# A two-layer hybrid backbone on one core: two tiles of tokens instead of one gather their experts in the second layer

## The chip, the core and the metric

The kernel runs on one core of a Trainium2 chip. The metric is the device time of one execution in microseconds (us); each time shown is the median of three timed runs. A separate execution is recorded by the hardware profiler, and all rows below come from that one.

## What is computed

Two layers over 512 latent tokens of width 1024, with 256 context tokens in front. Each layer has four mixers side by side (RG-LRU, RWKV-7, mLSTM, Hyena), then the expert part, PEER. The first layer computes context and latents (768 tokens), the second the latents alone (512 tokens). The change lies in the expert part of the second layer, which computes, cut to what matters:

```
def token_block(xb):                                   # h: the normed, modulated tokens
    q = (xb @ wq).reshape(T, 8, 2, 128)
    s = einsum('thcq,hckq->thck', q, keys)             # 8 heads, 2 halves, 128 keys each
    sv, si = top_k(s, 16)
    cand = sv[:, :, 0, :, None] + sv[:, :, 1, None, :] # 16 x 16 pairs of every head
    top_s, top_j = top_k(cand.reshape(T, 8, 256), 16)
    eidx = ...                                         # 8 x 16 = 128 experts of 16384 per token
    gate = softmax(top_s)
    act = gelu(einsum('td,thkd->thk', xb, U[eidx]))
    return einsum('thk,thkd->td', gate * act, V[eidx])
```

## The kernel before

Engines in short: PE is TensorE, DVE VectorE, ACT ScalarE, POOL GpSimd, SP the engine that only issues transfers. The second layer is `l = 1` in the code; every table of numbers has an entry for each layer, `X[l]`. A tile is 128 tokens; the second layer has four.

The expert part treats tokens in two ways.

- **Dense tiles.** All 16384 rows of U are multiplied with the tile's tokens on PE, in 128 products of 128 rows each (`s_part`), the gelu of the result goes to DRAM (`Ad`). A U product is: load 128 rows (`ur`), split them on ACT and DVE into a high and a low part (`uh`, `ul`), 24 matmuls (8 blocks of 128 features, 3 each for the parts), as many columns wide as there are dense tokens (`Wd`). The gates that routing chose are spread over all experts by `build` (comparisons and products on DVE, small matmuls on PE) and go to DRAM (`Gd`). Later come 128 V products: load `Ad`, `Gd` and 128 rows of V, multiply the first two (`gm`), split V and the result into high and low parts (`pv`), 24 matmuls into eight PSUM banks that gather over all 128 products.
- **Gathered tiles.** For each of the 128 experts of a token, a gather (an indirect DMA that POOL issues, line 1527) fetches row e of U for all 128 tokens into a buffer `grow` of 512 KB; DVE multiplies it with the tokens and sums (a U use, line 1500). Then 128 gathers fetch rows of V, and DVE adds each, times its weight, to a sum (a V use, line 244). A tile costs 256 gathers and 256 uses.

`choose(n, after)` paces the gathers. At each call it puts the uses of the rows whose call lies `LAG[l] = 2` calls back, then copies n columns of indices (`at`, on DVE), then issues n gathers, each into one of `GBUF[l]` buffers `grow`. The calls are laid in by hand: in `s_ahead` after each U product (`CHS`), in `build` (`CHN`), in `trailing` (`CHT`), and in the loop over V products, where n is what is left over the products that are left, until `CHE = 128`:

```
choose(min(8, (NS - done[0]) // max(1, CHE - j)), ins)
```

Before the change the second layer has `NG = 1` gathered tile, so three dense ones (384 columns), and `CUT = 0`: all 512 tokens are scored together (16 half heads, `scores`), then the gathered tile is routed first, then each dense tile is routed and built. `s_ahead(NSP[1][1] = 3)` puts three U products ahead of each quarter of a build; what is left of the 128 U products then runs in `trailing`, one gather beside each. The first layer has `NG = 2`, `CUT = 1` and 512 dense columns already: there the tokens are normed and scored in two pieces, the gathered tiles are scored and routed first, and the dense ones follow with gathers beside them.

The program's order on each engine comes from a scheduler at build time. Engines run their instructions in that order; a DVE instruction that waits holds up all behind it.

I call the stretch from the first routing matmul to the end of the U products the U stage, and what follows up to the end of the V products and uses the V stage.

Of the kernel before, what the change touches and what calls it, by code (L numbers as in the profile page):

```python
# [13 lines left out]
A = mybir.AluOpType  # L14
AF = mybir.ActivationFunctionType
X = mybir.AxisListType.X
PSUM, DRAM = bass.MemoryType.PSUM, bass.MemoryType.DRAM
# [3 lines left out]
EPS = 1e-6  # L21
# [5 lines left out]
# ---------------------------------------------------------------- layout on the host  # L27
# [90 lines left out]
def consts():  # L118
    o = {}
    for n, L in (("l", SEQ), ("c", CTX)):  # L120
        # Half of the times and of the frequencies: e and o below are the sums and differences of the tokens t and
        # their mirror images, of which the even and the odd frequencies need one each for cosine and sine.
        # 0: the filters, t against L - t; 1, 2: tokens, t + 1/2 against L - t - 1/2, and back.
# [73 lines left out]
NSP = ((5, 5, 6), (6, 3, 6))  # L197
# [8 lines left out]
GBUF = (4, 6)  # L206
CHN = (1, 6)
NG = (2, 1)
TOK = (2, 1)
CHS = ((1, 2), (200, 0))  # L210
CUT = (1, 0)
# [3 lines left out]
# ---------------------------------------------------------------- the program  # L215

def body(tc, I, out, dbg=None, stop=None):
# [56 lines left out]
    def segs(n):  # L274
        """columns in PSUM banks: the latents' 512, then the context's 256 before them"""
        return [(max(0, n - 512), n)] + ([(0, n - 512)] if n > 512 else [])

    with pool("keep") as kp, pool("scr", space=DRAM) as dp:
        # ---------------------------------------------------------- persistent
# [13 lines left out]
        def inv_sqrt(o, i, scale, eps_ap_or_val):  # L293
            """(i * scale + eps) ** -0.5"""
            act(o, i, AF.Ln, scale, eps_ap_or_val)
            act(o, o, AF.Exp, -0.5)
# [10 lines left out]
        # ---------------------------------------------------------- modulation vectors  # L307
        def ada(l, rounds, wp, pp, cs, dma, bufs):
            """columns 2048 * r on; the two vectors' products lie on partitions 32 * q and 32 * q + 1"""
# [23 lines left out]
        # ---------------------------------------------------------- Hyena's filters  # L333
        def dft_part(p, n, L, kind, f):
            """two parts each of the cosines and sines of 128 frequencies"""
# [6 lines left out]
        def sin_(p, t, ps, frq, bias, L):  # L342
            """sin(frq * (ps + bias)) with the argument brought to [-pi, pi]"""
# [13 lines left out]
        def spectrum(l, n, L, p, pp, dst_):  # L357
# [12 lines left out]
            # the first half of the times on the upper partitions; the second, mirrored and with the middle in the  # L370
            # place of time L, on the lower ones
# [10 lines left out]
            # forward plus and minus backward, each the sum (0) and difference (1) of a time and its mirror image  # L382
# [34 lines left out]
            # 1 / (L * (sum of the absolute values + EPS)); 1/L = 2/N is the weight of a frequency in the inverse  # L417
# [5 lines left out]
            for f in range(NC):  # L423
# [15 lines left out]
                if f == 0:  # L439
                    # the highest frequency, in the place of the sine of frequency 0  # L440
# [16 lines left out]
        # ---------------------------------------------------------- prologue  # L457
# [18 lines left out]
        # ---------------------------------------------------------- shared pieces  # L476
        def rms_scale(p, pp, srcs, n, tag, tags=(("sq", 2), ("rstd", 1))):
            """1 / sqrt(mean of squares over all rows + EPS), on every partition"""
# [14 lines left out]
        def norm_mod(hps, p, pp, x, l, which, t0, tag, cut=None):  # L493
            """what the products read, in two parts; for the tokens before and from cut on in a pool each"""
# [16 lines left out]
        def projector(wp, pp, src, tag, off=0, ks=range(8), eng=None):  # L511
            """rows of a product with h for the tokens from t0 on, by segments; early(c) fetches a row's weights"""
# [26 lines left out]
        def padded(p, zd, c, tag, bufs, t0):  # L539
            """a row block of z with two zeros before and one behind each stream, in three stretches of 256 tokens"""  # L540
# [12 lines left out]
        def conv(o, xp, taps, bias, t0):  # L553
            """o = sum of w * (token + shift) + bias; the first tap carries the bias"""
# [26 lines left out]
        # ---------------------------------------------------------- RG-LRU  # L581
# [1263 lines left out]
```

## Time and profile before

| | |
|---|---|
| median of three runs | 4984.07 us (4979.75 to 5007.8) |
| profiled execution, its span | 5021.4 us |
| expert part of the second layer in it | 3545 to 5005 us: U stage to 4437, V stage after it |
| busy over the span | PE 91%, DVE 72%, ACT 35%, POOL 27% |

The span runs from the first to the last instruction of the profiled execution; of that execution no other time is given. PE's busy time counts matmuls that overlap in the array, so it says that PE was rarely without one, not that it was at its peak. The share over the whole span mixes stages with different limits, so the stages of the expert part are read apart.

### The profile page before, as it was taken

How to read it: one execution, taken by the hardware profiler on the slowest of the kernel's cores; microseconds unless marked ns; L12 is line 12 of the kernel's file. 1: busy time of each engine (PE TensorE's matmuls, PEld its weight loads, DVE VectorE, ACT ScalarE, POOL GpSimd, SP SyncE). 2: the span in 40 equal slices, each digit the busy share in tenths (PEclk: the TensorE clock that was granted, in tenths of full speed). 3: DMA queues.
4: the chain of work that ended last, by engine and by line, in shares of the span. 5: the costliest groups of instructions: out<-in, count | busy, mean ns of one | idle time of the engine just before them, and what ended most of it. 6: DMA issues, size and time to landing. Idle time of an engine off the chain costs nothing. (4 is left out here: it accounts for less than half of the span.)

```text
span 5021.4 us, 66832 instructions
## 1 busy us (share of the span) xinstructions
PE 4590.8 (91%) x24203; PEld 3842.1 (77%) x24203; DVE 3624.9 (72%) x7303; ACT 1777.9 (35%) x2546; POOL 1375.8 (27%) x1117
## 2 busy tenths in 40 slices
PE   7879898799899999799999887898899998999998
PEld 3658567688777888687788665787688898999997
DVE  5772647399788897688889677556589875567777
ACT  4352222353233444322222335212534443333333
POOL 1211111002344454234455222000002332323332
PEclk9889999899999999899999898968999999999999
DMA  4442545346688999899999544203426889888896
GB/s 177 160 137 77 189 161 158 143 130 236 225 298 307 322 329 332 311 352 353 362 379 381 178 152 134 68 19 110 140 80 231 269 284 345 286 283 325 321 328 248
DMA packets 521083, 1170.01 MB, mean 233 GB/s; under 512 B 68192, under 2 KB 250272, under 8 KB 516272
## 3 DMA queue, kind: packets, MB, share of 16 engines
q1 hardware_dynamic: 227440, 563.42, 32.5%
q0 software_dynamic: 134912, 484.06, 27.2%
q10 hardware_dynamic: 158400, 118.25, 7.3%
q8 instruction: 191, 3.13, 0.3%
q14 instruction: 140, 1.15, 0.1%
HBM read 992.95 MB, written 173.02 MB: 232 GB/s over the span
## 5 line engine op out<-in xcount | busy, mean ns | idle before, releaser
L254 PE MATMUL d.S<-mrg.hhi,d.ul 128*128 128x512 f32 (+1 forms) x2048 | 772.6, 377 | 85.4 <-DVE d.ul L251 76.2
L1527 POOL DMA_INDIRECT d.grow<-in_V_dram,d.at x369 | 578.7, 1568 | 712.2 <-DVE d.at L1522 562.4
L254 PE MATMUL d.S<-mrg.hlo,d.uh 128*128 128x512 f32 (+1 forms) x2048 | 760.2, 371 | 0.1
L254 PE MATMUL d.S<-mrg.hhi,d.uh 128*128 128x512 f32 (+1 forms) x2048 | 757.6, 370 | 0.0
L254 PE MATMUL rt.O<-rt.pv,rt.pv 128*128 128x512 f32 (+1 forms) x2580 | 558.6, 366 | 41.5 <-DVE rt.pv L251 41.0
L254 PEld LDWEIGHTS rt.O<-rt.pv,rt.pv 128*128 128x128 f32 x2580 | 468.3, 189 | 108.8 <-issue 48.9
L254 PEld LDWEIGHTS d.S<-mrg.hhi,d.ul 128*128 128x128 f32 x2048 | 398.1, 194 | 144.5 <-DVE d.ul L251 94.7
L247 ACT ACTIVATE d.pa<-d.S 128x512 f32<-128x512 f32 (+1 forms) x256 | 139.7, 546 | 859.3 <-PE d.S L254 794.3
L254 PEld LDWEIGHTS d.S<-mrg.hlo,d.uh 128*128 128x128 f32 x2048 | 397.8, 194 | 39.2 <-DVE mrg.hlo L251 1.2
L254 PEld LDWEIGHTS d.S<-mrg.hhi,d.uh 128*128 128x128 f32 x2048 | 396.1, 193 | 41.4
L1527 POOL DMA_INDIRECT d.grow<-in_Ur_dram,d.at x233 | 302.9, 1300 | 433.2 <-DVE d.at L1522 326.8
L251 DVE TENSOR_TENSOR d.ul<-d.ur,d.uh 128x1024 fp32r<-128x1024 f32 x256 | 311.6, 1219 | 131.0 <-ACT d.uh L250 130.6
L1527 POOL DMA_INDIRECT rt.grow<-in_Ur_dram,rt.at x151 | 228.8, 1515 | 630.1 <-DVE rt.at L1522 569.4
L250 ACT CAST rt.pv<-rt.vr 128x1024 fp32r<-128x1024 f32 x172 | 181.1, 1053 | 588.0 <-DMA rt.vr<-in_V_dram 249.0
L1500 DVE SCALAR_TENSOR_TENSOR d.grow<-d.grow,rt.tok 128x1024 f32<-128x1024 f32 x233 | 281.9, 1221 | 121.6 <-DMA d.grow<-in_Ur_dram,d.at 120.8
L244 DVE SCALAR_TENSOR_TENSOR d.tok<-d.grow,rt.gw,d.tok 128x1024 f32<-128x1024 f32 x245 | 313.7, 1281 | 51.8 <-DMA d.grow<-in_V_dram,d.at 51.5
L254 PE MATMUL d.O<-rt.pv,rt.pv 128*128 128x512 f32 (+1 forms) x1548 | 337.5, 362 | 0.0
L254 PEld LDWEIGHTS d.O<-rt.pv,rt.pv 128*128 128x128 f32 x1548 | 280.7, 188 | 30.2
L254 PE MATMUL rt.O<-d.pv,d.pv 128*128 128x512 f32 (+1 forms) x1260 | 273.1, 365 | 8.1 <-DVE d.pv L251 7.2
L250 ACT CAST d.uh<-d.ur 128x1024 fp32r<-128x1024 f32 x256 | 267.5, 1046 | 27.7 <-issue 11.5
L254 PEld LDWEIGHTS rt.O<-d.pv,d.pv 128*128 128x128 f32 x1260 | 226.8, 188 | 44.1 <-issue 13.6
L254 PE MATMUL z.z<-hhi,z.wlo 128*128 128x512 f32 (+1 forms) x656 | 236.1, 360 | 23.5 <-POOL z.wlo L251 16.3
(619 smaller groups left out, 9380.0 us busy)
## 6 DMA issues: line engine op xcount, KB each, us to landing
d.ur<-in_U_dram SPq DMA_DIRECT2D x256, 512.0 KB, 5.2
rt.vr<-in_V_dram SPq DMA_DIRECT2D x256, 512.0 KB, 6.0
ada.adaw<-in_ada_w_dram POOLq DMA_DIRECT2D x80, 512.0 KB, 4.1
mrg.Ad<-d.pa ACTq DMA_DIRECT2D x128, 256.0 KB, 5.5
rt.gt<-mrg.Gd SPq DMA_DIRECT2D x32, 1024.0 KB, 9.4
rt.ga<-mrg.Ad SPq DMA_DIRECT2D x128, 256.0 KB, 6.9
mrg.Gd<-ro.x ACTq DMA_DIRECT2D x14, 2048.0 KB, 12.1
mrg.Gd<-rt.gst ACTq DMA_DIRECT2D x14, 2048.0 KB, 14.4
```

The lines of the kernel that those rows point to most:

```text
L244: return V.scalar_tensor_tensor(o, a, s, b, op0=op0, op1=op1)
L247: return S.activation(o, i, f, bias=bias, scale=scale)
L250: S.copy(hi, src)
L251: return (eng or V).tensor_tensor(lo, src, hi.bitcast(F32), op=A.subtract)
L254: PE.matmul(ps, l, r, start=start, stop=stop)
L1500: V.scalar_tensor_tensor(g, g, 1.0, s["h"], A.mult, A.mult, accum_out=w[:, e:e + 1])
L1527: G.indirect_dma_start(out=g, out_offset=None, in_=I["Ur"] if r % 256 < 128 else I["V"].rearrange("l j i d -> (l j i) d"), in_offset=bass. ...
```

## The change

Six tables of the second layer take the first layer's values or come near to them, and `NSP` puts ten U products instead of three ahead of each quarter of a build. (Comments are gone from the file as well; they are left out here.)

```
-NSP = ((5, 5, 6), (6, 3, 6))
+NSP = ((5, 5, 6), (6, 10, 6))
...
-GBUF = (4, 6)
-CHN = (1, 6)
-NG = (2, 1)
-TOK = (2, 1)
-CHS = ((1, 2), (200, 0))
-CUT = (1, 0)
+GBUF = (4, 4)
+CHN = (1, 1)
+NG = (2, 2)
+TOK = (2, 2)
+CHS = ((1, 2), (1, 2))
+CUT = (1, 1)
```

So in the second layer: two dense tiles (256 columns) instead of three; two gathered tiles, 512 gathers instead of 256; four `grow` buffers instead of six; two gathers after every U product instead of three at every step of 16 tokens of a build; the scores made in two pieces of 256 tokens, with the query weights loaded and split once for each.

What that does to the order is seen at three places on DVE. First the U products, late in the U stage. Before, one use and one copy of indices (`at`) stand with each split of a U block (`d.ul`), and the first V products (`gm` is gate times activation, `pv` their split parts) already stand between the last sixty U products:

```order
L1522 COPY rt.at_32296<-rt.ei_28713 128x1
L251 TENSOR_TENSOR d.ul_32303<-d.ur_32300,d.uh_32302 128x1024
L1500 SCALAR_TENSOR_TENSOR rt.grow_32257,rt.gw_28715<-rt.grow_32257,rt.tok_28207 128x1024
L1522 COPY rt.at_32335<-rt.ei_28713 128x1
L251 TENSOR_TENSOR d.ul_32342<-d.ur_32339,d.uh_32341 128x1024
L1500 SCALAR_TENSOR_TENSOR rt.grow_32298,rt.gw_28715<-rt.grow_32298,rt.tok_28207 128x1024
L1522 COPY rt.at_32374<-rt.ei_28713 128x1
L236 TENSOR_TENSOR rt.gm_5271_32203<-rt.ga_5263_32195,rt.gt_5266_32198 128x384
L251 TENSOR_TENSOR rt.pv_5281_32213<-rt.gm_5271_32203,rt.pv_5280_32212 128x384
L251 TENSOR_TENSOR rt.pv_5279_32211<-rt.vr_5268_32200,rt.pv_5278_32210 128x1024
```

Now two uses and a copy of two columns stand with each U product:

```order
L1500 SCALAR_TENSOR_TENSOR d.grow_30857,rt.gw_28385<-d.grow_30857,rt.tok_28136 128x1024
L1500 SCALAR_TENSOR_TENSOR d.grow_30859,rt.gw_28385<-d.grow_30859,rt.tok_28136 128x1024
L1522 COPY d.at_30939<-rt.ei_28383 128x2
L251 TENSOR_TENSOR d.ul_30948<-d.ur_30945,d.uh_30947 128x1024
L1500 SCALAR_TENSOR_TENSOR d.grow_30899,rt.gw_28385<-d.grow_30899,rt.tok_28136 128x1024
```

Each pair of uses has come in front of the split that PE needs for the next product.

Second, DVE in the V stage, one V product after the other. Before, one use stands with each product:

```order
L236 TENSOR_TENSOR rt.gm_5271_32203<-rt.ga_5263_32195,rt.gt_5267_32199 128x384
L244 SCALAR_TENSOR_TENSOR rt.tok_34520<-d.grow_38263,rt.gw_28715,rt.tok_34520 128x1024
L1522 COPY d.at_38333<-rt.ei_28713 128x1
L251 TENSOR_TENSOR d.pv_5722_34653<-rt.vr_5270_32202,d.pv_5721_34652 128x1024
L251 TENSOR_TENSOR d.pv_5724_34655<-rt.gm_5272_32204,d.pv_5723_34654 128x384
L236 TENSOR_TENSOR rt.gm_5272_32204<-rt.ga_5264_32196,rt.gt_5267_32199 128x384
```

Now two, and they work on rows that two calls before had asked for (`d.grow_39713` belongs to the call before `d.at_39750`, `d.grow_39752` to the call of `d.at_39750` itself):

```order
L1522 COPY d.at_39750<-rt.ei_28625 128x2
L251 TENSOR_TENSOR rt.pv_5959_35301<-rt.gm_5950_35292,rt.pv_5958_35300 128x256
L244 SCALAR_TENSOR_TENSOR d.tok_37981<-d.grow_39676,rt.gw_28627,d.tok_37981 128x1024
L251 TENSOR_TENSOR rt.pv_5961_35303<-rt.vr_5947_35289,rt.pv_5960_35302 128x1024
L236 TENSOR_TENSOR rt.gm_5949_35291<-rt.ga_5942_35284,rt.gt_5944_35286 128x256
L244 SCALAR_TENSOR_TENSOR d.tok_37981<-d.grow_39713,rt.gw_28627,d.tok_37981 128x1024
L1522 COPY d.at_39790<-rt.ei_28625 128x2
L251 TENSOR_TENSOR rt.pv_5963_35305<-rt.gm_5949_35291,rt.pv_5962_35304 128x256
L244 SCALAR_TENSOR_TENSOR d.tok_37981<-d.grow_39715,rt.gw_28627,d.tok_37981 128x1024
L251 TENSOR_TENSOR d.pv_5985_35408<-rt.vr_5948_35290,d.pv_5984_35407 128x1024
L236 TENSOR_TENSOR rt.gm_5950_35292<-rt.ga_5943_35285,rt.gt_5944_35286 128x256
L244 SCALAR_TENSOR_TENSOR d.tok_37981<-d.grow_39752,rt.gw_28627,d.tok_37981 128x1024
```

The use of a gathered row has moved in front of every split of V, and the parts that depend on dense tokens have narrowed from 384 to 256.

Third, DVE where the U stage ends, after the change: the last split of a U block, and what follows it:

```order
L251 TENSOR_TENSOR d.ul_35354<-d.ur_35351,d.uh_35353 128x1024
L244 SCALAR_TENSOR_TENSOR d.tok_32060<-d.grow_34867,rt.gw_28385,d.tok_32060 128x1024
L1522 COPY d.at_35031<-rt.ei_28383 128x2
L244 SCALAR_TENSOR_TENSOR d.tok_32060<-d.grow_34907,rt.gw_28385,d.tok_32060 128x1024
L244 SCALAR_TENSOR_TENSOR d.tok_32060<-d.grow_34909,rt.gw_28385,d.tok_32060 128x1024
```

It goes on with uses and copies alone, nine uses in all, and then comes the first `gm`. No U product is left to lie between, where 58 U splits stood behind the first `gm` before. Up to that `gm` DVE has now 253 uses behind it, where it had 134 by the end of the U products before; 259 uses remain for the V stage.

## Rows read from the trace of the kernel before

**Rows 1.** The page: its first line.

```profile
span 5021.4 us, 66832 instructions
```

**Rows 2.** Windows, second layer: us; busy (and count) by engine; granted clock, DMA, GB/s.

```profile
3545.00:3740.00 195.00, 181.69 (x816) 144.15 (x817) 127.44 (x557) 75.15 (x117) 0.00 (x0) 0.96 0.29 100
3740.00:4437.00 697.00, 644.90 (x3763) 629.86 (x3762) 506.27 (x958) 288.48 (x370) 202.02 (x135) 0.94 0.82 276
4437.00:5005.00 568.00, 554.80 (x3097) 536.45 (x3096) 439.52 (x634) 187.41 (x257) 199.01 (x122) 1.00 0.86 309
```

**Rows 3.** PE in order of time, 1010 to 1060 us: start, us, instruction.

```profile
1010.85 0.41 PE L254 MATMUL rt.q<-mrg.hlo,rt.whi 128*128 128x256 f32 x1
1011.07 0.41 PE L254 MATMUL rt.q<-mrg.hhi,rt.whi 128*128 128x256 f32 x1
...
1024.04 0.28 PE L254 MATMUL rt.q<-mrg.hhi,rt.whi 128*128 128x256 f32 x1
1024.16 0.39 PE L254 MATMUL d.S<-mrg.hhi,d.ul 128*128 128x512 f32 x1
```

**Rows 4.** Windows, first layer: part of its U stage, its V stage, 250 us thereof.

```profile
1250.00:2050.00 800.00, 758.71 (x3744) 628.32 (x3743) 680.51 (x1331) 307.49 (x378) 352.99 (x241) 0.97 0.88 303
2100.00:2800.00 700.00, 690.04 (x3001) 561.06 (x3000) 599.36 (x847) 196.72 (x251) 334.87 (x237) 1.00 0.97 362
...
2500.00:2750.00 250.00, 248.64 (x1088) 203.54 (x1087) 226.17 (x273) 70.77 (x90) 135.66 (x91) 1.00 1.00 381
```

**Rows 5.** Groups on DVE, 2110 to 2790 us: busy, mean ns | idle before, releaser.

```profile
L244 DVE SCALAR_TENSOR_TENSOR d.tok<-d.grow,rt.gw,d.tok 128x1024 f32<-128x1024 f32 x121 | 155.2, 1282 | 29.0 <-DMA d.grow<-in_V_dram,d.at 28.8
L1500 DVE SCALAR_TENSOR_TENSOR d.grow<-d.grow,rt.tok 128x1024 f32<-128x1024 f32 x109 | 132.3, 1222 | 55.7 <-DMA d.grow<-in_Ur_dram,d.at 55.5
...
L236 DVE TENSOR_TENSOR rt.gm<-rt.ga,rt.gt 128x512 f32<-128x512 f32 x121 | 83.7, 692 | 4.2
```

**Rows 6.** Groups on DVE, 1250 to 2050 us: the uses and the U splits.

```profile
L244 DVE SCALAR_TENSOR_TENSOR d.tok<-d.grow,rt.gw,d.tok 128x1024 f32<-128x1024 f32 x118 | 150.9, 1279 | 21.8 <-DMA d.grow<-in_V_dram,d.at 21.8
L251 DVE TENSOR_TENSOR d.ul<-d.ur,d.uh 128x1024 fp32r<-128x1024 f32 x106 | 129.0, 1217 | 30.4 <-ACT d.uh L250 30.2
L1500 DVE SCALAR_TENSOR_TENSOR d.grow<-d.grow,rt.tok 128x1024 f32<-128x1024 f32 x99 | 119.3, 1221 | 53.8 <-DMA d.grow<-in_Ur_dram,d.at 53.4
```

**Rows 7.** The tile rt.q: first and last start of its matmuls.

```profile
L254 PE MATMUL rt.q<-mrg.hhi,rt.wlo x384: 278/394/795, 1007.9 to 3736.6; 128*128 128x512 f32 x128, 128*128 128x256 f32 x64
```

**Rows 8.** The tile d.grow, 1124 to 2050 us: first gathers.

```profile
L1527 POOL DMA_INDIRECT d.grow<-in_Ur_dram,d.at x121: 932/942/2807, 1124.2 to 2043.8; - x121
```

**Rows 9.** Groups, 3500 to 5022 us: builds, gate times activation.

```profile
L236 DVE TENSOR_TENSOR rt.gm<-rt.ga,rt.gt 128x384 f32<-128x384 f32 x128 | 71.4, 558 | 8.1 <-DMA rt.gt<-mrg.Gd 2.9 <-DMA rt.ga<-mrg.Ad 1.0
...
L236 DVE TENSOR_TENSOR rt.og<-rt.o,rt.ijT 128x2048 f16<-128x2048 f16 x48 | 57.1, 1218 | 0.0
```

**Rows 10.** In order of time, 2600 to 2612 us: a gather's way in the V stage.

```profile
2602.64 0.16 DVE L1522 COPY d.at<-rt.ei 128x2 int32<-128x2 int32 x1
...
2603.07 0.94 POOL L1527 DMA_INDIRECT d.grow<-in_V_dram,d.at  x1 [1.46 <-DVE d.at L1522]
...
2604.72 1.67 POOL L1527 DMA_INDIRECT d.grow<-in_V_dram,d.at  x1 [0.71 <-DVE d.tok L244]
```

**Rows 11.** The tile d.grow, 2100 to 2810 us: issue to landing.

```profile
DMA to landing us min/median/max: 4.3/8.0/10.5
```

**Rows 12.** The tile d.grow, 4450 to 5000 us: issue to landing.

```profile
DMA to landing us min/median/max: 4.1/7.0/9.7
```

**Rows 13.** In order of time, 2046 to 2100 us: the first layer's change of stage.

```profile
2091.19 6.35 PE L254 MATMUL rt.O<-rt.pv,rt.pv 128*128 128x512 f32 x15 [27.35 <-DVE rt.pv L251]
```

**Rows 14.** DMA, 3545 to 5005 us: all, and the queue of the gathers.

```profile
DMA packets 170277, 387.32 MB, mean 265 GB/s; under 512 B 13520, under 2 KB 95568, under 8 KB 170046
...
q0 software_dynamic: 37008, 134.37, 24.9%
```

**Rows 15.** Windows, first layer: six us ahead of the first matmuls.

```profile
1005.00:1011.00 6.00, 3.67 (x10) 2.70 (x11) 5.29 (x8) 6.00 (x12) 0.00 (x0) 0.50 0.00 0
```

## The prediction, made before the changed kernel had run

> **What bounds the kernel now.** I read the windows by stage first, then the groups on VectorE (DVE), then the waits of the gathered rows. The profiled execution spans 5021.4 us [rows 1], 37.3 us more than the median of the timed runs; the sum below is made on its stages and its difference is put on the median, 4984.07 us. Only the second layer's expert part can move: 1460 us, of which 892 are the U stage and 568 the V stage [rows 2]. There TensorE (PE) sets the pace. In the V stage it is busy 554.8 of 568 us and starts 3097 matmuls, one every 183 ns; DVE is busy 439.5 us (77%), the DMA engines 86% [rows 2].
>
> Does PE gain from fewer columns? Matmuls of 256 columns start 0.12 us apart at the full clock [rows 3]. In the first layer's V stage, where they have 512, 3000 take 700 us, 233 ns each [rows 4]. So the price follows the columns, and 24 matmuls of 256 cost 2.9 us where those of 384 cost 4.4. PE loses a third of its work in U and V products, over 300 us: if it stayed the bound, the kernel would be clearly faster.
>
> It does not stay the bound. The first layer has run with two gathered tiles, four buffers and two gathers a product all along. Its V stage is the model: PE is full there (690 of 700 us), but DVE has no time left either. It is busy 599.4 us [rows 4], and its uses waited 29.0 + 55.7 us for rows to land in the 680 us that the groups cover [rows 5]; that is 98% of the time. Two loops are tight at once there, PE's and that of gathers and uses, and the change relieves PE's alone.
>
> **The sum, part by part.** *To the first gather.* In the first layer the first routing matmul starts at 1007.9 and the first gather at 1124.2, 116 us later [rows 7, 8]. Eight U products lie in between; with 256 instead of 512 columns they save 8 x 24 x 0.11 = 21 us, so 95 us: the first gather at 3640. DVE was busy 65% of the old first stretch [rows 2], so it does some 62 us of its work by then.
>
> *The rest of the U stage.* DVE's work in the old U stage is 127.4 + 506.3 = 634 us [rows 2]. It loses a tile's build, a third of four operations' 96 (32 x 1.218 = 39 us) [rows 9]. It gains 16 splits of query weights, of the form of the U splits at 1.217 us, 20 us [rows 6], 119 uses more (253 for 134, all of V's kind at 1.28 us, 152 us) and some 50 copies of indices at 0.16 (8 us) [rows 5, 10]. That makes 775, and 713 after the first gather. What share of the time can it reach? In the first layer's U stage it is busy 85.1% [rows 4], with 21.8 + 53.8 us of the rest waiting for gathered rows and 30.4 for ACT's cast ahead of the U splits [rows 6]. The best 250 us of the trace reach 90.5% [rows 4]. PE is no longer full, so I drop the casts' wait, which came when U buffers were freed late, and keep the gathers': 89.5%. 713 / 0.895 = 797, so the U stage ends at 4437: 0. At 85.1% it ends at 4478 (+41), at 95%, which no long stretch shows, at 4391 (-46).
>
> *The change of stage.* The first layer has no U product left to cover it: the V stage's first inputs wait for the last gates to be written, and PE stands idle for 27.35 us, waiting for DVE's first part of a V product [rows 13]. In the second layer this was hidden by the 58 U products behind the first `gm`. Now the order leaves only nine uses there, 12 us of work. I take half of the hole less than covered: 27 - 12 = 15, of which gathers that land meanwhile give back some: 8 us, bounds 0 and 27.
>
> *The V stage.* In the first layer a product takes 700 x 24 / 3000 = 5.6 us; DVE is busy 4.79 us of it and its uses wait 84.7 x 5.6 / 680 = 0.70 [rows 4, 5]. With 256 columns `gm` and the split beside it get cheaper: 692 ns at 512, 558 at 384 [rows 5, 9], so 0.27 us less each. Uses go from 237 / 125 = 1.9 [rows 4] to 259 / 128 = 2.02, +0.16. DVE's part is 4.41 us, and with the same wait a product takes 5.1.
>
> The loop of a buffer says the same from the other side. A use (1.28) [rows 5], the copy of indices (0.16), 0.27 us to the start of the gather on GpSimd [rows 10], and 8.0 us to landing [rows 11] are 9.7 us for the first gather of a pair; the second starts 1.65 us behind it [rows 10]. Since a row is used two calls after its gather and the four buffers hold just two calls, two products can't be shorter than 9.7 to 11.4 us: 4.9 to 5.7 a product. I take 5.1, 653 us for the stage: +85 on 568. Bounds: 4.41, DVE without a wait, 564 us (-4); 5.6 as in the first layer, 717 us (+149).
>
> *What else moves.* GpSimd issues 256 gathers more at about 1.5 us; in the first layer's V stage it was busy 335 of 700 us with as many [rows 4], so it is covered. The second scoring pass loads and multiplies the query weights again, but on half as many tokens each time: 768 matmuls at 0.12 us for 384 at 0.233, +3 us of PE's new slack. The copies of x, the mixers and the first layer are untouched.
>
> Sum: 0 + 8 + 85 = **+93 us on 5021.4**, so **5077 us** on the median, 1.9% slower. From the other end: 512 gathers from 3640 on, at 5.1 us for two, take 1306 us and end at 4946; the builds, routing and scoring, whose DVE work lies between, have to fit into the loop's waits or add some 150 us to it. The sum ends the V stage at 5005 + 93 = 5098, the upper end of that.
>
> **A rule on bandwidth.** The expert part moves 387.3 MB, 134.4 of them by gathers [rows 14]. It will move 134 MB more for the second gathered tile, 34 less of `Ad` and `Gd` (by their shapes) and 8 more of query weights: 496 MB. Some 20 pass before the first gather; 476 MB at the 381 GB/s of the first layer's best 250 us [rows 4] need 1249 us, at the 362 of its V stage 1315, so the transfers alone would end between 4889 and 4955, ahead of the sum. The Trainium skill, "DMA: Bandwidth & Descriptors", section "Specifications", puts the limit of HBM for one core at about 358 GB/s. The stretch at 381 is above it, so the row decides; by the rule the transfers would end at 4970, still ahead.
>
> **A rule on the clock.** PE will be idle some 2 us in each product. The granted clock in the stages is 0.94 to 1.00 [rows 2], and matmuls of 256 columns start 0.22 us apart at 1011 us [rows 3], in a stretch with the granted clock at 0.50 [rows 15], the lower of its two levels (1.2 of 2.4 GHz); PE was busy 3.67 of those 6 us. Cold throughout, a V product would take PE 24 x 0.22 = 5.3 us: the loop's time once more, +25 us over the stage at most. The Trainium skill, "TensorE: Matmul & The Clock Gate", section "Why this matters for your kernels", asks for TensorE to be kept continuously busy, since idle gaps bring the half clock back. It speaks against this change, but the price is bounded by the loop.
>
> **Rivals.** *Faster:* the loop is shorter than in the first layer, since less is moved for each product. For: rows landed 7.0 us after their issue in the old V stage [rows 12], which makes the first gather's loop 8.7 us, 4.4 a product; and DVE may reach 95% without PE in its way. V stage at 4.5: 576 us (+8), U stage -46, no hole: -38, 4946 us. Against: the old V stage loaded the DMA engines 86%, with half the gathers. It decides where a pair takes less than 4.5 us.
> *No change:* U stage at 90.5% (-9), V stage at 4.6 (+21), hole 0: about +12, 4996 us.
> *Much slower:* the gathers keep the first layer's pace, 5.6 us a product, and in the U stage 85.1%, with the hole in full: 41 + 27 + 149 = +217, 5201 us. For: DVE's order puts both uses ahead of the split that PE waits for, so every late row stalls both. Against: the first layer also had PE at its limit.
> *PE cold:* the clock at its lower level for most of the V stage adds up to 25 us to the forecast, 5102 us.
>
> **How the numbers follow.** A measurement can tell 0.5%, 25 us, from no change: 4959 to 5009. The forecast with the cold variant (5010 to 5165) holds 0.65, no change 0.15, faster 0.09, much slower 0.11. So slower 0.76, same 0.15, faster 0.09. The likeliest time is 5075 us. The range leaves out most of the faster case and of the much slower one: 4970 to 5165.
>
> **What would show it.** Right: in the V stage 24 matmuls of 256 columns take about 3 us and a product about 5; PE waits for DVE's `pv`, DVE's idle time is ended by landing rows, over 0.5 us a product; the U stage still ends near 4437; a gap of PE at the change of stage; DVE above 85% in both stages. Wrong: landing times below 7 us at two gathers a product; the U stage ending before 4390; or DVE with idle time that no gather ends, which would mean that another chain, such as ACT's casts or the loads, binds.

## The result and the profile after

The changed kernel takes 5259.59 us (median of 4 runs, 5246.21 to 5278.64), the kernel before 4985.45 beside it: 1.0531 times as long, 95% interval 1.0489 to 1.0573. The forecast was 5075 (4970 to 5165). The direction was right; the loss is three times the forecast's.

Windows of the changed kernel, columns as in [rows 2], from its first second-layer routing matmul: to the first gather, the rest of the U stage, the change of stage, the V stage's first half (U uses) and second half (V uses):

```profile
3588.00:3697.00 109.00, 102.93 (x797) 97.66 (x798) 103.67 (x420) 59.21 (x106) 0.54 (x2) 0.99 0.45 143
3697.00:4503.00 806.00, 537.90 (x3706) 517.00 (x3705) 628.09 (x1235) 247.47 (x349) 344.41 (x251) 0.81 0.83 284
4503.00:4531.00 28.00, 0.29 (x3) 0.09 (x1) 11.92 (x17) 3.29 (x5) 8.41 (x10) 0.55 0.97 348
4531.00:4892.00 361.00, 246.96 (x1526) 234.62 (x1527) 272.21 (x508) 92.20 (x126) 189.98 (x125) 0.81 0.90 320
4892.00:5224.00 332.00, 231.84 (x1543) 219.41 (x1543) 277.25 (x388) 86.26 (x127) 171.86 (x129) 0.88 0.95 348
```

Against [rows 2]: PE fell from over 90% busy to two thirds, and no engine took its place: DVE is busy 78% of the U stage and 75 and 84% of the V stage's halves; the DMA engines are at 0.83, 0.90 and 0.95. A product takes 24 matmuls, so the V stage's first half is 5.7 us a product (361 x 24 / 1526), its second 5.2. The waits of DVE say what it stood for; the lines above the dots are the U stage from 3697 to 4503, those below them the time from there to 5231:

```profile
DVE d.at L1522 <- DMA d.grow<-in_V_dram,d.at: 59.1, 25, 5.8
DVE d.grow L1500 <- DMA d.grow<-in_Ur_dram,d.at: 59.0, 50, 3.2
DVE d.ul L251 <- ACT d.uh L250: 18.1, 7, 6.6
DVE rt.grow L1500 <- DMA rt.grow<-in_Ur_dram,rt.at: 10.7, 4, 4.7
DVE d.tok L244 <- DMA d.grow<-in_V_dram,d.at: 9.8, 6, 4.5
DVE d.at L1522 <- DMA rt.grow<-in_V_dram,rt.at: 7.7, 4, 3.2
...
DVE d.grow L1500 <- DMA d.grow<-in_Ur_dram,d.at: 90.3, 83, 2.9
DVE rt.pv L251 <- ACT rt.pv L250: 26.0, 24, 1.9
DVE d.pv L251 <- ACT d.pv L250: 13.9, 12, 2.5
DVE d.tok L244 <- DMA d.grow<-in_V_dram,d.at: 13.2, 18, 2.1
```

The columns are us in total, times, longest. Rows on their way (the releaser is a gather into a `grow` buffer) ended 146 us of waits in the U stage, 79 of them at uses and 67 at the copies of indices, and 104 us behind it, at uses. PE stands behind them: these are its waits from 4531 to 5231, 146 us ended by DVE's splits of V products (the 28 us of the change of stage among them) and 96 by ScalarE's casts.

```profile
PE rt.O L254 <- DVE rt.pv L251: 107.7, 40, 27.9
PE rt.O L254 <- ACT rt.pv L250: 62.3, 32, 3.3
PE rt.O L254 <- DVE d.pv L251: 38.0, 18, 5.2
PE rt.O L254 <- ACT d.pv L250: 33.7, 17, 4.0
```

The two halves of the V stage differ. In the first, from 4531 to 4892, rows ended 88 us of DVE's waits, and DVE's splits ended 137 us of PE's waits (with those 28), the casts 4. In the second, from 4892 to 5231, rows ended 15 us of DVE's waits, and the casts ended 92 us of PE's, the splits 8; the casts themselves stood 92 us for loads of V and 118 for TensorE to be done with `pv`. So in the V stage the late rows set the pace of the first half only; in the second, PE stands behind the casts.

One turn of the loop in the first half, in order of time, 4700 to 4714 us:

```profile
4700.72 0.17 DVE L1522 COPY d.at<-rt.ei 128x2 int32<-128x2 int32 x1
...
4701.16 2.00 POOL L1527 DMA_INDIRECT d.grow<-in_Ur_dram,d.at  x1 [2.15 <-DVE d.at L1522]
...
4703.47 0.94 POOL L1527 DMA_INDIRECT d.grow<-in_Ur_dram,d.at  x1 [0.30 <-issue]
...
4705.01 1.23 DVE L1500 SCALAR_TENSOR_TENSOR d.grow<-d.grow,rt.tok 128x1024 f32<-128x1024 f32 x1 [2.32 <-DMA d.grow<-in_Ur_dram,d.at]
...
4706.76 1.23 DVE L1500 SCALAR_TENSOR_TENSOR d.grow<-d.grow,rt.tok 128x1024 f32<-128x1024 f32 x1 [0.52 <-DMA d.grow<-in_Ur_dram,d.at]
...
4707.91 0.17 DVE L1522 COPY d.at<-rt.ei 128x2 int32<-128x2 int32 x1
4707.99 0.42 DVE L251 TENSOR_TENSOR rt.pv<-rt.gm,rt.pv 128x256 fp32r<-128x256 f32 x1
...
4708.46 2.50 PE L254 MATMUL rt.O<-rt.pv,rt.pv 128*128 128x256 f32 x10 [4.01 <-DVE rt.pv L251]
...
4709.89 1.23 DVE L1500 SCALAR_TENSOR_TENSOR d.grow<-d.grow,rt.tok 128x1024 f32<-128x1024 f32 x1
...
4712.74 1.23 DVE L1500 SCALAR_TENSOR_TENSOR d.grow<-d.grow,rt.tok 128x1024 f32<-128x1024 f32 x1 [1.62 <-DMA d.grow<-in_Ur_dram,d.at]
...
4713.90 0.16 DVE L1522 COPY d.at<-rt.ei 128x2 int32<-128x2 int32 x1
```

The two gathers of the call at 4700.72 are used after the next call (4707.91), at 4709.89 and 4712.74. The second starts at 4703.47 and its use, which waited, at 4712.74: 9.3 us from issue to use, 12.0 from the copy of its index. Only behind that use stand the next copy (4713.90), the next two gathers and the split on which PE waits.

### The profile page after: what moved, and what is told of

Its sections match the earlier page's. It is cut to its first block, busy times and chain, and to the rows that moved or that the text cites. A ratio compares the mean times of both kernels' runs of the same rounds, so it can differ in the third digit from the quotient of the medians.

```text
span 5258.3 us, 68137 instructions
## 1 busy us (share of the span) xinstructions
PE 4391.9 (84%) x24344; PEld 3649.2 (69%) x24344; DVE 3880.1 (74%) x7773; ACT 1744.9 (33%) x2555; POOL 1689.7 (32%) x1374
## 5 line engine op out<-in xcount | busy, mean ns | idle before, releaser
L1527 POOL DMA_INDIRECT d.grow<-in_V_dram,d.at x498 | 725.3, 1456 | 703.4 <-DVE d.at L1522 322.8
L254 PE MATMUL d.S<-mrg.hhi,d.ul 128*128 128x512 f32 (+1 forms) x2048 | 744.3, 364 | 234.8 <-DVE d.ul L251 220.7
L1527 POOL DMA_INDIRECT d.grow<-in_Ur_dram,d.at x468 | 639.9, 1367 | 806.0 <-DVE d.at L1522 636.5
L1500 DVE SCALAR_TENSOR_TENSOR d.grow<-d.grow,rt.tok 128x1024 f32<-128x1024 f32 x468 | 569.1, 1223 | 265.5 <-DMA d.grow<-in_Ur_dram,d.at 260.3
L254 PE MATMUL d.S<-mrg.hlo,d.uh 128*128 128x512 f32 (+1 forms) x2048 | 728.6, 356 | 0.1
L254 PE MATMUL d.S<-mrg.hhi,d.uh 128*128 128x512 f32 (+1 forms) x2048 | 724.1, 354 | 0.0
L244 DVE SCALAR_TENSOR_TENSOR d.tok<-d.grow,rt.gw,d.tok 128x1024 f32<-128x1024 f32 x494 | 632.4, 1280 | 74.8 <-DMA d.grow<-in_V_dram,d.at 73.7
L254 PEld LDWEIGHTS d.S<-mrg.hlo,d.uh 128*128 128x128 f32 x2048 | 427.0, 208 | 38.8 <-DVE mrg.hlo L251 0.9
L254 PEld LDWEIGHTS d.S<-mrg.hhi,d.uh 128*128 128x128 f32 x2048 | 425.2, 208 | 40.5
L251 POOL TENSOR_TENSOR z.wlo<-z.wraw,z.whi 128x1024 fp32r<-128x1024 f32 x48 | 122.2, 2548 | 429.4 <-ACT z.whi L250 407.5
```

The costliest lines, as they stand in the source:

```text
L244: return V.scalar_tensor_tensor(o, a, s, b, op0=op0, op1=op1)
L251: return (eng or V).tensor_tensor(lo, src, hi.bitcast(F32), op=A.subtract)
L254: PE.matmul(ps, l, r, start=start, stop=stop)
L1500: V.scalar_tensor_tensor(g, g, 1.0, s["h"], A.mult, A.mult, accum_out=w[:, e:e + 1])
L1527: G.indirect_dma_start(out=g, out_offset=None, in_=I["Ur"] if r % 256 < 128 else I["V"].rearrange("l j i d -> (l j i) d"), in_offset=bass. ...
```

## Experiments

Times are medians, and ratios (with 95% interval) are to the kernel before, timed on the same chip beside it; a ratio can lie up to 0.7% beside the quotient of the two medians, so differences of a few tens of us between experiments are rough. Each diff is cut, and is against the changed kernel unless it says otherwise. "Theory A" is the loop of a buffer (from a use over the next gather to its landing), B the DMA engines' bandwidth, C VectorE's work.

**A longer loop.**

```diff
-LAG = (2, 2)
-GBUF = (4, 4)
+LAG = (2, 3)      # e1; e2: (2, 4)
+GBUF = (4, 6)     # e1; e2: (4, 8)
```

> Six buffers for gathered rows in the second layer instead of four, and a row is used three calls after its gather instead of two. Theory A (the loop of a buffer, from a use over the next gather to its landing, sets the pace of both stages): the 59 + 11 + 88 us of waits for rows in the changed kernel go, a product of the V stage falls from 5.47 us to DVE's own 4.4 to 4.7, some 100 us less there, and 60 to 100 us less in the U stage: about 5060 to 5110 us. Theory B (the DMA engines' bandwidth, 332 GB/s at a share of 0.92 in the V stage, binds): the bytes are the same, so the time stays within 25 us of 5259. Theory C (VectorE's work binds): the same work, so it stays within 25 us as well.

> Eight buffers, a row used four calls after its gather. Theory A: as with six buffers and up to 30 us further, 5030 to 5110 us, since landing times are not all alike; then DVE's 4.4 us of work a product is the next bound and no further buffer helps. Theory B and theory C: within 25 us of 5259.

Measured: 5146.05 us, 1.0279 (1.0197 to 1.0361), and 5119.65 us, 1.0236 (1.0162 to 1.0310). Both are clearly faster than the changed kernel with the same bytes and the same work, so neither B nor C alone sets its pace; but 113 us came where A expected 150 to 200, and 140 where it expected 150 to 230. With eight buffers the waits of the uses are gone (under 3 us in the U stage), and the copies of indices wait in the U stage as before (69 us, 67 in the changed kernel): each of the three index tiles is free only when the gathers of three calls back are done with it.

In the V stage only the first half gained. These are its halves with eight buffers, 4.4 us a product (296 x 24 / 1600) instead of 5.7, and 5.2 as in the changed kernel:

```profile
4484.00:4780.00 296.00, 228.69 (x1600) 217.58 (x1601) 270.84 (x515) 89.94 (x132) 137.74 (x124) 0.90 1.03 399
4780.00:5096.00 316.00, 214.32 (x1472) 202.97 (x1471) 261.73 (x367) 82.33 (x122) 159.41 (x122) 0.89 0.93 345
```

> The changed kernel with six buffers for rows instead of four, as before the change, while a row is still used two calls after its gather. If the number of buffers was the limit: as much less as with six buffers and three calls, 5120 to 5160 us. If the distance in calls is the limit (a gather's indices are copied behind the uses of two calls before, so no gather can start earlier however many buffers are free): within 25 us of 5259.

Measured: 5218.23 us, 1.0467 (1.0367 to 1.0568): 41 us less, between the two expectations; the interval overlaps the changed kernel's, and DVE's waits for rows in the V stage are the same (88.8 and 12.7 us). So it is mainly the distance of two calls, which both kernels have, and not the cut from six buffers to four; that the cut cost nothing is not shown.

> Eight buffers for rows, a row used four calls after its gather, and six index tiles instead of three (with three, the copy of the indices in one call waits until the gathers of three calls before have read theirs: 64 us of such waits in the U stage of the run with eight buffers). Theory A: these waits go, 40 to 64 us less than that run's 5120: 5055 to 5080; the V stage stays at 4.8 us a product, since there the loads of V's blocks are now late, not the rows. Rival (the rows are late because the DMA engines are behind, so that the wait only moves from the index copy to the use or to the casts): 5100 to 5125.

Beside the tables of e2:

```diff
-                    at = T(gp, [128, 8], I32, "at", 3)
+                    at = T(gp, [128, 8], I32, "at", (3, 6)[l])
```

Measured: 5098.33 us, 1.0169 (1.0101 to 1.0237), not told apart from e2. The waits of the index copies went (69 to 10 us), but those for ScalarE's casts of U rose from 24 to 64: the rival came true in the main. Waits of DVE in this kernel's U stage (3714 to 4436 us), of ACT in its V stage (4467 to 5097), and windows of the U stage behind the first gather and the V stage's halves:

```profile
DVE d.ul L251 <- ACT d.uh L250: 64.2, 26, 11.2
...
DVE d.at L1522 <- DMA d.grow<-in_V_dram,d.at: 10.0, 5, 5.5
DVE d.grow L1500 <- DMA d.grow<-in_Ur_dram,d.at: 5.8, 8, 2.1
...
ACT rt.pv L250 <- DMA rt.vr<-in_V_dram: 170.8, 54, 5.9
...
ACT d.pv L250 <- DMA rt.vr<-in_V_dram: 97.9, 28, 6.4
```

```profile
3714.00:4436.00 722.00, 512.85 (x3709) 494.84 (x3707) 621.62 (x1244) 248.73 (x351) 377.39 (x256) 0.83 0.89 320
...
4467.00:4770.00 303.00, 232.86 (x1656) 221.14 (x1656) 276.37 (x524) 93.20 (x137) 148.10 (x128) 0.92 1.02 398
4770.00:5083.00 313.00, 208.59 (x1418) 198.59 (x1419) 254.42 (x353) 79.05 (x116) 155.17 (x118) 0.88 0.91 337
```

In the V stage the casts wait for loads of V, and in its first half the DMA engines are at a share of 1.02, 398 GB/s. In the U stage, at a share of 0.89, only 6 us of ScalarE's waits ahead of a cast of U were ended by a load; 78 us (33 in the changed kernel) were ended by stores of `Ad`, ahead of the gelus on the same engine.

**Less of one suspect.** The changed kernel with half the columns in each use, and with half of each row gathered:

```diff
-stt(s["y"], g, w[:, e:e + 1], s["y"])                    # e3; U uses alike
+stt(s["y"][:, :512], g[:, :512], w[:, e:e + 1], s["y"][:, :512])
...
-G.indirect_dma_start(out=g, in_=src, ...)                # e4
+G.indirect_dma_start(out=g[:, 0:512], in_=src.rearrange("e (a d) -> (e a) d", a=2), ...)
```

> Leaves out half of each use in the second layer: the products of U and the sums over V take 512 of a row's 1024 columns, the gathers still bring whole rows into four buffers. Theory C (VectorE's work): some 508 uses shrink by about 0.6 us each, 300 us less: about 4960 us. Theory A (the loop of a buffer, of which a pair's uses are two times 1.28 of some 11 us): 1.2 us less in each loop of two products, 0.6 us for each of some 256 products, 100 to 160 us less: 5100 to 5160. Theory B: within 25 us of 5259.

> Gathers only 2 KB of each 4 KB row in the second layer (another half row than the reference's), and the uses read these 512 columns twice, so that VectorE's work and the number of gathers stay. Theory B (bandwidth): 134 MB less of some 496 at 332 GB/s: 350 to 400 us less, down to where DVE's or PE's work binds, about 4950. Theory A: a gather lands sooner, by perhaps 2 of 8 us, so that a product gets 1 us shorter in both stages: 120 to 220 us less, 5040 to 5140. Theory C: within 25 us of 5259.

Measured: 5041.76 us, 1.0101 (1.0061 to 1.0141), and 5060.70 us, 1.0136 (1.0072 to 1.0201). Each takes some 200 us. For short uses (218 us less) that is more than A expected and less than C; for half rows (199) it is within what A expected and half of what B did. A shorter use and a sooner landing both shorten the loop, and each also relieves VectorE or the transfers. With short uses DVE still waits 162 us for rows in the U stage and 149 in the V stage (4416 to 5003 us), and the DMA engines are at a share of 1.01 there; with half rows its uses wait under 2 us in the U stage (the copies of indices 64) and 8 in the V stage. A gather of half a row lands in 4.8 us (median, 3700 to 4450 us) and 5.3 (4500 to 5100); in e1, with whole rows, these are 7.6 and 8.2.

**What binds once the loop is open.** e6 has half rows, e9 half rows and half uses, both with eight buffers and six index tiles (the edits are those of e4, of e3 and of e5):

> The kernel with eight buffers and six index tiles, and only half of each row gathered (another half row than the reference's; the uses read it twice). If, with the loop open, bandwidth is what binds next, VectorE's work of 624 and 540 us at some 95% gives a U stage of about 665 and a V stage of about 565 us behind the first gather: 4960 to 4990 us. If VectorE's work or another chain binds already in the run with whole rows, no more than 25 us below that run.

> The kernel with eight buffers and six index tiles, gathering half rows and using only these 512 columns (the products and sums over the other half of each row are left out in the second layer). If VectorE's work is what bound the run with half rows and whole uses (95% busy in its U stage, 92% in its V stage), 300 us less of it make 200 to 250 us: about 4750 to 4800 us. If TensorE's chain or ScalarE's casts bind there, no more than 80 us come: above 4910.

Measured: 4995.97 us, 1.0016 (0.9979 to 1.0054), and 4829.55 us, 0.9661 (0.9598 to 0.9724). Windows of the two, the U stage behind the first gather and the V stage's halves:

```profile
3675.00:4326.00 651.00, 493.20 (x3706) 476.98 (x3704) 619.96 (x1242) 247.91 (x350) 380.61 (x257) 0.87 0.79 255
...
4346.00:4640.00 294.00, 219.56 (x1608) 207.87 (x1608) 271.47 (x516) 94.05 (x136) 160.69 (x126) 0.95 0.84 291
4640.00:4925.00 285.00, 203.35 (x1466) 190.97 (x1466) 261.89 (x367) 81.05 (x119) 166.80 (x122) 0.95 0.79 271
```

```profile
3712.00:4327.00 615.00, 493.06 (x3708) 475.41 (x3707) 502.28 (x1264) 246.74 (x350) 346.54 (x266) 0.89 0.81 273
...
4343.00:4570.00 227.00, 208.22 (x1617) 201.18 (x1618) 203.53 (x511) 92.07 (x134) 154.24 (x124) 0.98 1.01 377
4570.00:4791.00 221.00, 192.17 (x1453) 182.45 (x1453) 197.49 (x366) 84.19 (x120) 182.89 (x119) 0.97 0.97 346
```

So fewer bytes help once the loop is open: 102 us from e5 to e6 (76 by the ratios), which ends 6 us above its range. They don't help where the queues were fullest: the first half of the V stage takes 4.4 us a product in both (303 x 24 / 1656 and 294 x 24 / 1608), though the share fell from 1.02 to 0.84; VectorE is busy 91 and 92% there. The gain lies in the U stage (722 to 651 us) and in the V stage's second half (5.3 to 4.7 us a product), at shares of 0.89 and 0.91. That the bandwidth as such is the bound there, and not the time to landing or the order of casts and stores, isn't shown.

VectorE's work is the next bound in the V stage: less of it brings the halves from 4.4 and 4.7 us a product to 3.4 and 3.7. In the U stage, where e6 has VectorE busy 95%, 118 us less work give 36 us. Together it is another 166 us, somewhat less than expected. Even with the loop open and half the bytes, two gathered tiles are only level with one.

**TensorE and the change of stage.**

```diff
-mm(ps[:, :b - a], vh[:, ks], al[:, a:b], False, False)   # e10: V products; U products alike
-mm(ps[:, :b - a], vh[:, ks], ah[:, a:b], False, stop and i == n - 1)
+mm(ps[:, :b - a], vh[:, ks], al[:, a:b], False, stop and i == n - 1)
...
-NSP = ((5, 5, 6), (6, 10, 6))                            # e7
+NSP = ((5, 5, 6), (6, 3, 6))
```

> The changed kernel without the third matmul (high part by high part) of the U and V products of the second layer: 16 matmuls a product instead of 24. Theory A: TensorE waits for the loop, so the time stays within 25 us of 5259. Rival (TensorE's lower granted clock, 0.81 to 0.88 in these stages, has made it the bound again): TensorE's 1017 us of busy time fall by about 330, and 80 us or more come off.

> The changed kernel with 3 U products ahead of each half build instead of 10, as before, so that some 58 of them stand behind the builds and cover the change of stage. If the 28 us in which TensorE had nothing are the price of the change of stage: 5225 to 5240 us. If the loop of the buffers sets the time of both stages, the gathers go no faster and the gap only turns into waits elsewhere: within 25 us of 5259.

Measured: e10 5307.42 us, 1.0642 (1.0590 to 1.0694); e7 5315.31 us, 1.0617 (1.0574 to 1.0660). A third less of TensorE's matmuls brings nothing, so its work isn't the bound; the test is weaker than planned, since the granted clock fell to 0.73 and 0.68 in the two stages and TensorE's busy time by some 160 us instead of 330. In e7 V products stand between the last U products, and the gap of 28 us is gone (TensorE's longest wait from 4500 to 4700 is 9.7 us); yet 56 us were lost (43 by the ratios). With three U products ahead of each quarter build the calls, and with them the gathers, come slower during the builds: 237 rows had been used by the end of the U products (4544) against 248 by 4503, and the V stage took the rest at the loop's pace. Both expectations missed e7; the one that the gap is a price of its own isn't borne out, but as e7 slows the gathers too, what closing the gap alone would bring is not shown. E10's 48 us more missed its expectations too.

**One tile, and the order.**

```diff
-NG = (2, 2)                                              # e8, TOK alike
+NG = (2, 1)
...
-CHS = ((1, 2), (1, 2))                                   # e12: e8 and, beside GBUF 6 and NSP 3 as before,
+CHS = ((1, 2), (2, 1))
-CHN = (1, 1)
+CHN = (1, 2)
```

> One tile of 128 tokens gathers, as before, but it is routed ahead of the others, with the changed kernel's four buffers and two gathers a U product. Theory A: the gathers are done early in the V stage, which TensorE then paces with 24 matmuls of 384 columns, some 560 us; the U stage gets 120 uses more at the pace of the loop, some 60 to 90 us longer than before: 5010 to 5090 us, so that more than half of the loss comes from the second tile. Rival (the new order and its pacing cost, not the second tile): over 5150.

> One gathered tile routed ahead of the others, its 256 gathers spread over both stages: one for every second U product, one for every call in the builds, the rest in the V stage, U products left behind the builds as before. If the loss of one tile routed ahead (2.5% with two gathers a U product) came from crowding all gathers into the U stage, the V stage takes its 555 us again and the U stage, whose products start beside the routing, no more than before: 4930 to 5000 us. If the routing ahead itself costs (a second pass over the query weights, two sets of scores): above 5060.

Measured: e8 5147.69 us, 1.0251 (1.0174 to 1.0327); e12 5053.99 us, 1.0122 (1.0071 to 1.0172). E8 lies just below the rival's bound (5150) and above theory A's range. All its gathers fall into the U stage, which takes 923 us for 825; TensorE then does little for 68 us, and the V stage, without a gather, takes 534. Spread out, the V stage takes 559 again, and the U stage 895, between the two expectations.

> The kernel before with two gathered tiles that are routed last, as its one tile was, with eight buffers for rows and its own pacing of the calls. The U stage loses a build and some routing work, but only some 120 rows are used before its end, and the V stage gets three gathers a product: 3 x 1.28 us and 2.3 us of VectorE's other work, 6.2 to 6.6 us a product, 790 to 850 us: about 5200 to 5300 us, no better than the changed kernel. If routing ahead is where the change loses, it is below 5150.

```diff
 (against the kernel before)
-GBUF = (4, 6)
-NG = (2, 1)                                              # TOK alike
+GBUF = (4, 8)
+NG = (2, 2)
-order = [] if CUT[l] else [NT - 1]
+order = [] if CUT[l] else list(range(NT - 1, ND - 1, -1))
```

Measured: 5161.93 us, 1.0312 (1.0239 to 1.0384), better than the changed kernel and than was expected, and 12 us above the bound that would have put the loss on routing ahead. A product takes 6.1 us, but with three rows in it, 2.0 us a row against the changed kernel's 2.7: six rows are on their way instead of four. Its V stage is full of transfers:

```profile
4740.00:5120.00 380.00, 243.03 (x1504) 228.29 (x1503) 338.67 (x505) 85.65 (x123) 245.11 (x188) 0.84 1.00 381
```

**The longer loop without the second tile.**

```diff
 (against the kernel before: e13)                         # e14: e12 with LAG 4, GBUF 8, six index tiles
-LAG = (2, 2)
-GBUF = (4, 6)
+LAG = (2, 3)
+GBUF = (4, 9)
-at = T(gp, [128, 8], I32, "at", 3)
+at = T(gp, [128, 8], I32, "at", (3, 6)[l])
```

> The kernel before with nine buffers for rows instead of six, a row used three calls after its gather instead of two, and six index tiles. If the loop is a cost of the change alone, because in the kernel before TensorE sets the pace and VectorE's 185 us of waits for rows lie beside it: within 25 us of the kernel before. TensorE waited 36 us in the U stage and 12 in the V stage for VectorE's parts; if the late rows are behind these waits, up to 45 us less: 4940 to 4965. If the loop costs the kernel before as much as the changed one: 100 us less or more.

> One gathered tile routed ahead, its gathers spread over both stages, now with eight buffers, a row used four calls after its gather, and six index tiles. If the loop made the U stage 895 us long (VectorE waited some 140 us in it for rows, TensorE 83 us for VectorE), it comes down to TensorE's 802 us and a few per cent: 820 to 850 us, in all 4980 to 5020 us, level with the kernel before. If the second scoring pass and the new order cost by themselves, it stays above 5035.

Measured: e13 4944.80 us, 0.9930 (0.9892 to 0.9967), a version that beats both kernels, if by little; e14 4989.55 us, 0.9985 (0.9949 to 1.0021), level with before. In e13 DVE's waits for rows are all but gone (4 us), and TensorE doesn't wait in the V stage:

```profile
4408.00:4940.00 532.00, 532.00 (x3071) 532.00 (x3070) 438.45 (x624) 183.29 (x251) 115.46 (x122) 1.00 0.91 330
```

So the loop, with the index tiles, cost the kernel before some 49 us (35 by the ratio) and the changed one 161 (e5; 180 by the ratios). Of e12's loss the longer loop gives back 64 us. Routing ahead is then no loss against the kernel before, but no gain over e13 either.

## Why the prediction was wrong

The mechanism named as the sum's second way, the loop of a buffer, is what happened in the U stage and in the first half of the V stage. The sum took it at too low a price, put a wait of the U stage at nothing, and started the U stage too early.

**To the first gather (3640).** It came at 3697. The stage was taken to start at 3545, but in the trace before, the second layer's first routing matmul starts at 3612.9, and what lay between was still the mixers' output product and the norm; after, it starts at 3588.3 (tile rt.q from 3500 to 3900 us, before and after):

```profile
L254 PE MATMUL rt.q<-mrg.hhi,rt.wlo x128: 392/398/795, 3612.9 to 3736.6; 128*128 128x512 f32 x128
...
L254 PE MATMUL rt.q<-mrg.hhi,rt.wlo x256: 277/282/508, 3588.3 to 3869.6; 128*128 128x256 f32 x128
```

This was a misread boundary, and with 68 us it is the largest single error. The 95 us from the first routing matmul were 109. The 25 us by which the changed kernel's trace comes earlier to this point have nothing to do with the change: the mixers' last product already comes 24 us earlier, and nothing ahead of it was changed.

**The rest of the U stage (0).** It ended at 4503, 66 us later than forecast (68 + 14 for the start and 9 for its length, less those 25). From the first gather it took 806 us where 797 were reckoned, but by two errors that cancel, which is luck: DVE's work was 628 us, not 713, and its share 78%, not 89.5%. Of the work, 104 us and not 62 were done before the first gather, and 22 of the 634 belonged to the stretch ahead of the stage. The step that failed here is the share of 89.5%, which kept the waits of the uses for their rows and no others. Those waits came as expected: 79.5 us of 806, where the groups of [rows 6] have 75.6 of 800. The copies of indices were put at nothing, as they are next to nothing in the first layer (waits of DVE there, 1250 to 2050 us), and here they waited 67 us:

```profile
DVE rt.at L1522 <- DMA d.grow<-in_V_dram,d.at: 2.9, 3, 1.2
DVE d.tok L244 <- DMA rt.grow<-in_V_dram,rt.at: 2.3, 1, 2.3
DVE d.at L1522 <- DMA d.grow<-in_V_dram,d.at: 1.7, 1, 1.7
```

The rest of the 178 us of idle time is 25 for casts, whose wait the prediction dropped, and small waits. (With the casts' wait dropped, the rows give 88.9%, not 89.5: 85.1 and 30.4 of 800.) That TensorE's wider products stretch the calls apart in the first layer, and so hide part of the loop, is argued from this and was not tried; nor were more index tiles alone in the changed kernel.

**Change of stage (+8).** 28 us, as in the first layer [rows 13]: the nine uses, taken to cover half of it, covered none. In e7, where it is covered, no time was gained.

**V stage (+85).** From its first matmul to the last use it took 700 us instead of 653. The step that failed is the price of the loop: it gave 4.9 us a product for the first gather of a pair and 5.7 for the second, and 5.1 was taken. Both uses stand ahead of the next index copy, so the later gather decides, and 5.7 is what the first half took: some 37 of the 47 us. The second half, with 5.2, came out near 5.1 by luck: DVE waited there 15 us for rows and 40 for casts, PE waited 92 us for casts, and e1, e2 and e5, whose loop is longer, take 5.2 to 5.3 there as well. The prediction had named this as a sign of being wrong: "idle time that no gather ends". "DVE's part is 4.41 us, and with the same wait" was close on DVE (549 / 128 = 4.3 us) and too low on the wait (0.70 us a product; 103 us for rows and 40 for casts, of 700, are 1.1).

From the first routing matmul to the end, the traces differ by 262 us, where 93 were forecast. The 169 us between are 68 for the boundary, 14 up to the first gather, 9 in the U stage, 20 at the change of stage, 47 in the V stage and 11 behind it. Against the medians 184 are missing: of the 37 us by which the profiled execution of before lay above its median, 25 lay ahead of this point and 12 behind it, and 3 are rounding and the changed kernel's own median.

**Rivals.** *Much slower*, with 0.11, was nearest: 5.6 a product and the first layer's U stage, +217, where the traces differ by 237 from end to end. Its V stage is right for the first half; its U stage (85.1% of DVE) is not, and the misread boundary is in it too. *PE cold* was right on the clock (0.81 to 0.88); whether it cost the 25 us that it allowed, no run shows. *Faster* stands refuted. Its sign, landing under 7 us, can't be read in the changed kernel's trace, which has no landing times; in e1 the medians are 7.6 and 8.2 us.

**The two rules.** The transfers were said to end ahead of the sum, and in the changed kernel they aren't what binds. Halving the gathered bytes gives 102 us once the loop is open (e5, e6), but none of it in the stretch with the most traffic, 398 GB/s. The Trainium skill, "Perfetto Trace Analysis", section "Roofline", says that a single core can pull more than its share of 358 GB/s, up to some 435 of its 16 DMA engines; the 398 agree. As to the clock, TensorE with a third of its time idle was granted 0.81 to 0.88 of full speed, and with 16 instead of 24 matmuls 0.73 and 0.68 in the two stages. The Trainium skill, "TensorE: Matmul & The Clock Gate", section "Why this matters for your kernels", warns that idle gaps bring the lower clock back; the trace agrees. What the lower clock cost here isn't shown: in e10 TensorE's work and its clock fell together, and the time rose by 48 us.

**Open.** Why e10 is slower than the changed kernel by some 48 us wasn't settled. In its V stage the casts ended 257 us of TensorE's waits (96 in the changed kernel), and the casts waited 265 us for loads of V (119) and 234 for matmuls (185); slower matmuls may hold `pv` longer. What sets the 5.2 us a product of the V stage's second half, where PE stands behind the casts, was not tried by itself, nor what bounds e9's U stage.

## What to carry to other kernels

When work is moved from a full engine to a loop of transfers and uses, price the loop by the row that comes last: add up index copy, issue, landing and every use that stands ahead of the next copy, and divide by the calls between gather and use. If that exceeds what the old bound took, the loop is the new bound, and it can be so with no engine full: look for an engine that waits often and briefly for the same transfer. Read each stage, and each half of a stage, by itself: here the late rows ended the waits in the U stage and in half of the V stage, and casts in the other half. Then lengthen the distance between a gather and its use, with buffers for rows and for indices to match, and only then ask whether the added bytes and the added work fit at all; here they didn't.

## What the hardware showed that was not expected

The 16 DMA engines carried 398 GB/s over 303 us (e5), above the 381 of [rows 4], and with half the gathered bytes the same products took the same 4.4 us (e6): a share of 1.02 alone didn't show a bound. In the turn shown, a gather's row was used 9.3 us behind its issue in the changed kernel, where landing took 8.0 (median) in the first layer [rows 11]. Fewer matmuls made the kernel no faster and lowered the granted clock: in e10's V stage from 4537 to 5259,

```profile
4537.00:5259.00 722.00, 421.20 (x2046) 380.74 (x2047) 550.94 (x898) 172.38 (x255) 355.26 (x253) 0.68 0.90 320
```

2046 matmuls were busy 421 us (206 ns each), where 3069 took 479 in the changed kernel (156 ns).
